# Two changes in a network of two blocks: leftover U blocks spread over the V pass, and both halves of the feed-forward activations side by side in one matmul

## The chip, the cores and the metric

The kernel runs on one core of a Trainium2 chip. The metric is the time of one execution on the device in microseconds (us). The profile is one execution taken by the hardware profiler. Engines are named as in it: PE is TensorE (matmuls; PEld its weight loads), DVE is VectorE, ACT is ScalarE, POOL is GpSimd, and SP is the engine whose queue issues most DMAs.

## What is computed

Two blocks follow one another on 256 tokens of width 1024 (the first also carries 256 context tokens in its first layer). All data is fp32.

```python
# first block, per layer (2): attention / Fourier / convolution mixer, then a PEER layer
def peer_ffn(h, w_query, sub_keys, u_tab, v_tab):      # 16384 experts, 8 heads, top 16
    ...
    s_top, i_top = lax.top_k(s, PEER_TOPK)
    ...
    best, pos = lax.top_k(cand, PEER_TOPK)
    gate = jax.nn.softmax(best, axis=-1)
    u = jnp.take(u_tab, eid, axis=0)
    act = jax.nn.gelu(jnp.einsum('chkd,cd->chk', u, hc)) * gate
    v = jnp.take(v_tab, eid, axis=0)
    return jnp.einsum('chk,chkd->cd', act, v)

# second block, per layer (2): swiglu, attention mixer, swiglu, each with norms and modulation
def swiglu(h, w_gate, w_up, w_down):                   # width 2816
    return (jax.nn.silu(h @ w_gate) * (h @ w_up)) @ w_down
```

## The kernel before

**Products in three parts.** fp32 operands are split into a high half (the value as fp32r, rounded) and a low half (the remainder). `split` (L338) does it for weights: ACT copies `raw` to `wh` (L339), DVE or POOL subtracts to give `wl` (L340). `mm3` (L369) then makes three matmuls per 128 x 128 weight block: high weight with high activation (L371), high weight with low activation (L372), low weight with high activation (L373). Weights come as pieces of 8 blocks, 512 KB, loaded by `raw` (L344) on SP's queue; four raw tiles and two of each half rotate. `linear` (L375) runs such products over output blocks m, accumulates in a PSUM tile of 512 columns of which it uses the first n, and calls `evac` for each.

**The PEER layer** (`peer`, L1181) does not gather rows for all tokens: it multiplies all experts densely and masks. In layer 0 there are 512 tokens; the first 128 are done by gathered rows (`rows_up` L1151, `rows_down` L1167, on POOL's queue and DVE), the other 384 densely. A U block is 512 experts: four quarters of 8 weight blocks, 24 matmuls of 384 columns each, with a Gelu on ACT into `a4` (two buffers in pool `pp`). While the U blocks run, the top-k search `topk` (L989) for four tiles of 128 tokens is advanced by a generator. Each of its steps has a cost; for each quarter of a U block `peer` pays it `budget` units (3.1 in layer 0) and lets it run till they are spent. Its costs: 1.0, 16 x 1.1, 4.0, 8 x 0.7, 32 x 0.75 for every tile, and 2.0 and 32 x 1.7 more for a tile that is done densely (one-hot products, tiles `oa` and `ob` on DVE, `sc` on PE, `stg` on POOL). The rows of the first tile advance by `rate["up"]` (1.22) per quarter once that tile's search is done. A block's result is written to DRAM (`ad`, ACT's queue, L1269), the gates to `gd` (L1133).

The search ends in block number nb - 1; blocks from nb on are left. The loop's own sums give 122 quarters, hence nb = 31 in layer 0.

**The V pass** follows. `prep(b)` reads the gates of block b (L1288, 768 KB in layer 0, as much as its `a`) and either reads its `a` back from DRAM (L1293, b < nb) or computes the U block there and then, multiplies, and splits the product into `w4h` and `w4l`. V blocks are then taken two at a time (`deep` = 2), eight output blocks d of 8 weight blocks (24 matmuls) each, from weights `vt`. Order of the blocks: the first one left over, then all others in their order. `prep` runs two to four blocks ahead. POOL's part of the weight splits is switched off in this pass (`self.share = 0`). `rows_down` advances by 1.15 steps for each d. The program order is only a priority: the framework's scheduler lays out each engine's order ahead of time, and each engine then runs its own list in order.

**Feed-forward** (`ffn`, L1452), four times: 44 output blocks (gate and up alternating) of 8 weight blocks, then 8 output blocks of 22. `e` takes Silu of a gate block straight from PSUM (L1463), multiplies with the up block from PSUM (L1466) and splits the product into `ah` and `al` (L1467, L1468). `out_evac` (L1394) squares and scales each output block from PSUM. In layer 0 `sums` adds modulation sums on DVE (L443), 1.4 per pair of blocks.

Of the kernel before, what the change touches and what calls it, by code (L numbers as in the profile page):

```python
# [12 lines left out]
F32R = mybir.dt.float32r  # L13
U32 = mybir.dt.uint32
I32 = mybir.dt.int32
AF = mybir.ActivationFunctionType
# [217 lines left out]
class Kernel:  # L234
# [134 lines left out]
    def mm3(self, out, wh, wl, xh, xl, start, stop):  # L369
        mm = self.nc.tensor.matmul  # L370
        mm(out, wh, xh, start=start, stop=False)  # L371
        mm(out, wh, xl, start=False, stop=False)  # L372
        mm(out, wl, xh, start=False, stop=stop)  # L373

# [611 lines left out]
    rate = {("gate", 0): (10, 0, 2), ("gate", 1): (4, 0, 2), ("u", 0): 0, ("u", 1): 0, ("v", 0): 0, ("v", 1): 1.25, "mix": (5, 1.3), "up": 1.22, "down": 1.15, "ffn": 1.4, "out": 1, "att": (0.4, 0.4), "norm": ((4,4), (2,2), (4,4), (4,4))}  # L986
# [194 lines left out]
    def peer(self, l, budget):  # L1181
# [8 lines left out]
        with ExitStack() as es:  # L1190
# [90 lines left out]
            with self.pool(f"vp{l}") as vp:  # L1281
# [59 lines left out]
                if nb < 32:  # L1341
                    order = [nb] + order[:nb] + order[nb + 1 :]
# [27 lines left out]
    def hidden(self):  # L1370
        h = self.h = self.t(self.bp, [P, 2, 8, T], "h", F32R, bufs=1)
        self.rhs = (lambda k: h[:, 0, k], lambda k: h[:, 1, k])
        return h
# [78 lines left out]
    def ffn(self, l, j, nxt):  # L1452
        nc = self.nc
        with self.banks(mm=4, sc=3), self.pool(f"fp{l}{j}") as fp:
            ah = self.t(fp, [P, NF, T], "ah", F32R)
            al = self.t(fp, [P, NF, T], "al", F32R)
# [3 lines left out]
            def e(m, ps):  # L1460
                if m % 2 == 0:
                    sg["t"] = self.t(fp, [P, T], "sg", bufs=2)
                    nc.scalar.activation(sg["t"], ps, AF.Silu)  # L1463
                else:
                    t, k = sg["t"], m // 2
                    nc.vector.tensor_tensor(t, ps, t, op=OP.mult)  # L1466
                    nc.scalar.activation(ah[:, k], t, AF.Copy)  # L1467
                    last = nc.vector.tensor_sub(al[:, k], t, ah[:, k].bitcast(F32))  # L1468
                    self.sums(self.rate["ffn"], last)
                if m == 12 and l == 0 and j == 0:  # L1470
                    self.bias_read()

            self.linear(gu, 8, range(2 * NF), self.rhs, e, lead=4)
            if l == 0 and j == 1:
                self.sums_end()
            st = self.out_begin(l, 2 * j, True)
            self.linear(
                self.stream("wdn", (2 * l + j) * NF), NF, range(8), (lambda k: ah[:, k], lambda k: al[:, k]),
                lambda d, ps: self.out_evac(st, d, ps, nxt is None),
# [177 lines left out]
    def run(self):  # L1657
# [13 lines left out]
        self.peer(0, 3.1)  # L1671
# [39 lines left out]
```

## Time and profile before

| | |
|---|---|
| median of 3 runs | 4171.94 us (4168.49 to 4172.41) |
| the profiled execution | 4176.94 us, span of its instructions 4175.2 us |
| mean granted clock of TensorE | 0.945 |
| PE busy | 3820.4 us (92%) |
| DVE busy | 3235.8 us (77%) |
| ACT busy | 1794.7 us (43%) |
| POOL busy | 968.9 us (23%) |
| DMA | 944.96 MB, mean 226 GB/s |

Where stages lie, in us from the span's start: first mixer to 490, PEER layer 0 about 500 to 1937 (U blocks and search to 1330, V pass from there), second mixer to 2200, PEER layer 1 to 3050, then the second block. Busy time of PE is modelled, and matmuls overlap by their pipeline, so the distance between the starts of two matmuls is their cost, not the duration of one. A row of waits says which engine and line waited for which.

### The profile page before, as it was taken

What the parts mean: (1) busy time and instruction counts of PE and PEld (TensorE: products, weight loads), DVE (VectorE), ACT (ScalarE), POOL (GpSimd) and SP (SyncE); (2) the same over time, 40 slices, a digit from 0 to 9 for tenths busy, and PEclk for the clock granted to TensorE, in tenths of its full rate; (3) what the DMA queues carried; (4) which work ended last, traced back from release to release, by engine and by line L of the source; (5) the groups of instructions that cost most, each with busy time, mean ns of one, the idle gap of its engine ahead of it and who ended that gap; (6) DMA issues with size and microseconds to landing.
All of it is one profiled execution on the core that took longest, in us unless ns stands there. A gap on an engine that the chain in (4) does not pass through costs nothing.

```text
span 4175.2 us, 69284 instructions
## 1 busy us (share of the span) xinstructions
PE 3820.4 (92%) x25443; PEld 3562.4 (85%) x25443; DVE 3235.8 (77%) x7950; ACT 1794.7 (43%) x2986; POOL 968.9 (23%) x803
## 2 busy tenths in 40 slices
PE   7889898978897699999899999999989989999898
PEld 5568798978786599998689999999989879998798
DVE  4768778988987699996768997898868778656664
ACT  3342333433444233333344656444444554444543
POOL 0100014654634233440302848000000010100100
PEclk9999999999896799999899999999999989999899
DMA  5436548888756999984235767999869439554244
GB/s 181 157 103 216 184 156 292 290 287 279 251 191 176 254 348 345 340 324 140 98 117 186 251 234 254 378 363 341 310 232 315 155 104 320 159 184 146 95 162 142
DMA packets 331123, 944.96 MB, mean 226 GB/s; under 512 B 30832, under 2 KB 118512, under 8 KB 330784
## 3 DMA queue, kind: packets, MB, share of 16 engines
q1 hardware_dynamic: 201776, 722.15, 49.8%
q0 software_dynamic: 38272, 137.38, 10.3%
q10 hardware_dynamic: 90736, 81.01, 5.9%
q8 instruction: 201, 3.29, 0.3%
q14 instruction: 138, 1.13, 0.1%
HBM read 855.23 MB, written 85.19 MB: 225 GB/s over the span
## 4 chain that ended last, share of the span: by engine, by line
PE 46%; DVE 8%; issue 7%; DMA 3%; ACT 1%; POOL 1%; another core or an unknown queue 1%; ACTq 0%; SPq 0%; DVEq 0%; POOLq 0%
PE mm L373 14%; PE mm L371 14%; PE mm L372 14%; DVE wl L340 2%; DMA raw<-in_vt 2%; DVE cj L1061 1%; ACT wh L339 1%; PE sc L1122 1%; DMA arow<-in_adat 1%; DMA gd<-stg 1%; DVE cacc L770 1%; DVE w4l L340 0%; DVE nu L535 0%; PE sc L510 0%
## 5 line engine op out<-in xcount | busy, mean ns | idle before, releaser
L339 ACT ACTIVATE wh<-raw 128x1024 fp32r<-128x1024 f32 x946 | 997.0, 1057 | 1535.0 <-PE mm L372 1173.3
L340 DVE TENSOR_TENSOR wl<-raw,wh 128x1024 fp32r<-128x1024 f32 x840 | 1054.6, 1259 | 446.4 <-ACT wh L339 439.2
L373 PE MATMUL mm<-h2h,wl 128*128 128x256 f32 (+2 forms) x2176 | 694.5, 320 | 61.6 <-DVE wl L340 57.2
L371 PE MATMUL mm<-h2h,wh 128*128 128x256 f32 (+2 forms) x2176 | 692.7, 320 | 20.7 <-ACT a L1238 13.8
L372 PE MATMUL mm<-h2l,wh 128*128 128x256 f32 (+2 forms) x2176 | 692.2, 318 | 0.0
L371 PE MATMUL mm<-w4h,wh 128*128 128x384 f32 (+1 forms) x2048 | 631.8, 312 | 26.0 <-ACT wh L339 25.8
L373 PE MATMUL mm<-w4h,wl 128*128 128x384 f32 (+1 forms) x2048 | 601.2, 312 | 35.2 <-DVE wl L340 35.1
L372 PE MATMUL mm<-w4l,wh 128*128 128x384 f32 (+1 forms) x2048 | 630.3, 311 | 2.3 <-DVE w4l L340 2.3
L371 PE MATMUL mm<-h,wh 128*128 128x256 f32 x1712 | 498.4, 291 | 16.5 <-ACT h L540 6.7
L372 PE MATMUL mm<-h,wh 128*128 128x256 f32 x1712 | 494.4, 289 | 2.4 <-DVE h L541 1.8
L373 PE MATMUL mm<-h,wl 128*128 128x256 f32 x1712 | 490.7, 287 | 0.5 <-DVE wl L340 0.5
L373 PEld LDWEIGHTS mm<-h2h,wl 128*128 128x128 f32 x2176 | 425.4, 196 | 74.1 <-DVE wl L340 65.3
L371 PEld LDWEIGHTS mm<-h2h,wh 128*128 128x128 f32 x2176 | 425.4, 196 | 27.8 <-ACT a L1238 16.6
L372 PEld LDWEIGHTS mm<-h2l,wh 128*128 128x128 f32 x2176 | 425.4, 196 | 2.7
L373 PEld LDWEIGHTS mm<-w4h,wl 128*128 128x128 f32 x2048 | 383.3, 191 | 42.1 <-DVE wl L340 41.8
L371 PEld LDWEIGHTS mm<-w4h,wh 128*128 128x128 f32 x2048 | 391.3, 192 | 31.2 <-ACT wh L339 30.2
L372 PEld LDWEIGHTS mm<-w4l,wh 128*128 128x128 f32 x2048 | 391.5, 191 | 2.8 <-DVE w4l L340 2.8
L371 PEld LDWEIGHTS mm<-h,wh 128*128 128x128 f32 x1712 | 335.5, 196 | 24.2 <-ACT h L540 10.4
L372 PEld LDWEIGHTS mm<-h,wh 128*128 128x128 f32 x1712 | 335.2, 196 | 9.7 <-DVE h L541 7.1
L340 POOL TENSOR_TENSOR wl<-raw,wh 128x1024 fp32r<-128x1024 f32 x106 | 260.2, 2455 | 345.2 <-ACT wh L339 332.1
L373 PEld LDWEIGHTS mm<-h,wl 128*128 128x128 f32 x1712 | 334.9, 196 | 0.7 <-DVE wl L340 0.7
L1146 POOL DMA_INDIRECT vr<-in_vg,rowid x128 | 196.0, 1531 | 375.3 <-DVE racc L1178 350.6
(356 smaller groups left out, 7413.0 us busy)
## 6 DMA issues: line engine op xcount, KB each, us to landing
raw<-in_ut SPq DMA_DIRECT2D x256, 512.0 KB
raw<-in_vt SPq DMA_DIRECT2D x256, 512.0 KB
raw<-in_wgu SPq DMA_DIRECT2D x176, 512.0 KB
arow<-in_adat SPq DMA_DIRECT2D x144, 512.0 KB
raw<-in_wdn SPq DMA_DIRECT2D x88, 512.0 KB
gd<-stg ACTq DMA_DIRECT2D x20, 2048.0 KB
raw<-in_win SPq DMA_DIRECT2D x66, 512.0 KB
raw<-in_wmod SPq DMA_DIRECT2D x48, 512.0 KB
```

The lines of the kernel that those rows point to most:

```text
L339: self.nc.scalar.activation(h, src, AF.Copy)
L340: (eng or self.nc.vector).tensor_sub(l, src, h.bitcast(F32))
L371: mm(out, wh, xh, start=start, stop=False)
L372: mm(out, wh, xl, start=False, stop=False)
L373: mm(out, wl, xh, start=False, stop=stop)
L770: nc.vector.scalar_tensor_tensor(av[:, cc], u[:, cc, :, k : k + T], w[:, cc * 31 + k : cc * 31 + k + 1], av[:, cc], op0=OP.mult, op1=OP.add,)
L1061: nc.vector.scalar_tensor_tensor(junk, self.iota[:, :NCAND], pf[:, h, k : k + 1], eid[:, h, :], op0=OP.is_equal, op1=OP.mult, accum_out=se ...
L1122: nc.tensor.matmul(pg[:, j * 256 : (j + 1) * 256], oa[:, 2 * h + j], obs[h][:, j].rearrange("p a b -> p (a b)"), start=True, stop=True,)
L1146: self.nc.gpsimd.indirect_dma_start(out=r, out_offset=None, in_=self.A[table], in_offset=bass.IndirectOffsetOnAxis(ap=ids[:, i : i + 1], a ...
```

## The change

It has two parts, and three numbers go with them.

In the PEER layer with gathered rows (layer 0) the budget per quarter goes from 3.1 to 3.9 and the rows' rate from 1.22 to 1.65. The blocks that are left when the search ends are no longer taken as "the first of them, then all in order", but sorted by their share of progress, so that they lie evenly among the others: with nb = 25 the order is 25, 0, 1, 2, 3, 26, 4, 5, 6, 7, 27, 8 and so on. Layer 1 keeps its order and its budget.

In the feed-forward networks the high and the low half of an activation block lie beside each other, [k, 2, T]. One matmul of 512 columns multiplies the high weight with both, another of 256 columns adds the low weight's product to the first half. Two halves of the PSUM tile result, and `halves` adds them: a copy of the second on ACT, an addition on DVE. Silu, the multiplication and `out_evac` then read this sum from SBUF.

```diff
+    def linear2(self, get, nk, ms, rhs, evac, lead=1):
+
+        ms = list(ms)
+        mm = self.nc.tensor.matmul
+        for grp in [ms[:lead]] + [[m] for m in ms[lead:]]:
+            pss = [self.ps("mm") for _ in grp]
+            for k in range(nk):
+                both = rhs[:, k].rearrange("p a b -> p (a b)")
+                for m, ps in zip(grp, pss):
+                    wh, wl = get(m * nk + k)
+                    mm(ps, wh, both, start=k == 0, stop=False)
+                    mm(ps[:, 0:T], wl, rhs[:, k, 0], start=False, stop=k == nk - 1)
+            for m, ps in zip(grp, pss):
+                evac(m, ps)
+
+    def halves(self, out, ps):
+        self.nc.scalar.activation(out, ps[:, T : 2 * T], AF.Copy)
+        self.nc.vector.tensor_tensor(out, ps[:, 0:T], out, op=OP.add)
+        return out
...
-    rate = {("gate", 0): (10, 0, 2), ("gate", 1): (4, 0, 2), ("u", 0): 0, ("u", 1): 0, ("v", 0): 0, ("v", 1): 1.25, "mix": (5, 1.3), "up": 1.22, "down": 1.15, "ffn": 1.4, "out": 1, "att": (0.4, 0.4), "norm": ((4,4), (2,2), (4,4), (4,4))}
+    rate = {("gate", 0): (10, 0, 2), ("gate", 1): (4, 0, 2), ("u", 0): 0, ("u", 1): 0, ("v", 0): 0, ("v", 1): 1.25, "mix": (5, 1.3), "up": 1.65, "down": 1.15, "ffn": 1.4, "out": 1, "att": (0.4, 0.4), "norm": ((4,4), (2,2), (4,4), (4,4))}
...
                 order = list(range(32))
-                if nb < 32:
+                if g0:
+                    order.sort(key=lambda b: ((b - nb) / (32 - nb), 0) if b >= nb else (b / nb, 1))
+                elif nb < 32:
                     order = [nb] + order[:nb] + order[nb + 1 :]
...
     def hidden(self):
-        h = self.h = self.t(self.bp, [P, 2, 8, T], "h", F32R, bufs=1)
-        self.rhs = (lambda k: h[:, 0, k], lambda k: h[:, 1, k])
+        t = self.hh = self.t(self.bp, [P, 8, 2, T], "h", F32R, bufs=1)
+        h = self.h = t.rearrange("p k a b -> p a k b")
+        self.rhs = (lambda k: t[:, k, 0], lambda k: t[:, k, 1])
         return h
...
-            ah = self.t(fp, [P, NF, T], "ah", F32R)
-            al = self.t(fp, [P, NF, T], "al", F32R)
+            a2 = self.t(fp, [P, NF, 2, T], "a2", F32R)
+            ah, al = a2[:, :, 0], a2[:, :, 1]
...
                 if m % 2 == 0:
-                    sg["t"] = self.t(fp, [P, T], "sg", bufs=2)
-                    nc.scalar.activation(sg["t"], ps, AF.Silu)
+                    t = sg["t"] = self.halves(self.t(fp, [P, T], "sg", bufs=2), ps)
+                    nc.scalar.activation(t, t, AF.Silu)
                 else:
                     t, k = sg["t"], m // 2
-                    nc.vector.tensor_tensor(t, ps, t, op=OP.mult)
+                    u = self.halves(self.t(fp, [P, T], "su", bufs=1), ps)
+                    nc.vector.tensor_tensor(t, u, t, op=OP.mult)
...
-            self.linear(gu, 8, range(2 * NF), self.rhs, e, lead=4)
+            self.linear2(gu, 8, range(2 * NF), self.hh, e, lead=4)
...
-            self.linear(
-                self.stream("wdn", (2 * l + j) * NF), NF, range(8), (lambda k: ah[:, k], lambda k: al[:, k]),
-                lambda d, ps: self.out_evac(st, d, ps, nxt is None),
+            self.linear2(
+                self.stream("wdn", (2 * l + j) * NF), NF, range(8), a2,
+                lambda d, ps: self.out_evac(st, d, self.halves(self.t(fp, [P, T], "su", bufs=1), ps), nxt is None),
             )
...
-        self.peer(0, 3.1)
+        self.peer(0, 3.9)
```

## Rows read from the trace of the kernel before

**Rows 1.** The page's slices: busy tenths of two engines in 40 equal slices.
```profile
PE   7889898978897699999899999999989989999898
DVE  4768778988987699996768997898868778656664
```

**Rows 2.** Busy by stretch: length, PE, PEld, DVE, ACT, POOL, PEclk, DMA, GB/s.
```profile
500.00:545.00 45.00, 43.80 (x200) 36.06 (x201) 23.34 (x70) 17.00 (x29) 0.00 (x0) 0.97 0.22 71
...
690.00:765.00 75.00, 69.79 (x382) 68.75 (x383) 63.32 (x295) 22.70 (x34) 33.09 (x26) 0.95 0.87 306
765.00:880.00 115.00, 102.88 (x592) 98.52 (x591) 114.29 (x220) 59.95 (x101) 89.69 (x94) 0.97 0.89 302
880.00:1030.00 150.00, 119.63 (x626) 116.06 (x625) 120.70 (x563) 42.45 (x61) 62.79 (x49) 0.87 0.76 263
1030.00:1150.00 120.00, 102.73 (x536) 96.01 (x535) 116.07 (x207) 52.90 (x92) 78.52 (x81) 0.90 0.79 260
...
1243.00:1312.00 69.00, 51.36 (x126) 35.42 (x127) 68.14 (x155) 38.15 (x66) 46.43 (x63) 0.53 0.41 126
...
1330.00:1440.00 110.00, 61.73 (x292) 57.58 (x291) 55.18 (x90) 22.91 (x36) 21.31 (x13) 0.77 0.97 236
1440.00:1880.00 440.00, 432.68 (x2465) 426.21 (x2464) 413.69 (x624) 152.53 (x207) 166.79 (x110) 1.00 0.93 340
...
500.00:1312.00 812.00, 708.99 (x3655) 663.75 (x3656) 713.85 (x2755) 324.27 (x510) 380.62 (x360) 0.90 0.69 233
```

**Rows 3.** Groups by line, DVE's and POOL's weight splits in 500:1312.
```profile
L340 DVE TENSOR_TENSOR wl<-raw,wh 128x1024 fp32r<-128x1024 f32 x91 | 131.0, 1440 | 38.3 <-ACT wh L339 34.2 <-PE sc L1122 3.7
...
L340 POOL TENSOR_TENSOR wl<-raw,wh 128x1024 fp32r<-128x1024 f32 x41 | 98.5, 2402 | 171.1 <-ACT wh L339 160.3 <-PE sc L1122 6.5 <-PE mm L373 3.9
```

**Rows 4.** DVE's waits in 545:1312: who for whom, total us, times, longest.
```profile
DVE ur L1159 <- DMA ur<-in_ug,rowid: 30.3, 15, 6.4
DVE top L1006 <- ACT s L1001: 16.9, 3, 10.5
DVE wl L340 <- ACT wh L339: 15.8, 15, 2.9
```

**Rows 5.** Order of time, PE, middle of the V pass: start, duration, engine, line.
```profile
1601.05 0.33 PE L373 MATMUL mm<-w4h,wl 128*128 128x384 f32 x1
...
1602.09 0.33 PE L373 MATMUL mm<-w4h,wl 128*128 128x384 f32 x1
```

**Rows 6.** DMA queues and issues in 1320:1420 (packets, MB, share), and a chain step.
```profile
q0 software_dynamic: 2728, 7.96, 60.5%
...
a<-ad SPq DMA_DIRECT2D x4, 768.0 KB
...
1335.11 38.05 DMA raw<-in_vt
```

**Rows 7.** Order of time, PE: 256 columns in feed-forward, 512 in the first mixer.
```profile
4140.08 0.28 PE L371 MATMUL mm<-ah,wh 128*128 128x256 f32 x1
...
4141.49 0.28 PE L371 MATMUL mm<-ah,wh 128*128 128x256 f32 x1
...
69.65 0.39 PE L371 MATMUL mm<-hs,wh 128*128 128x512 f32 x1
...
72.37 0.39 PE L371 MATMUL mm<-hs,wh 128*128 128x512 f32 x1
```

**Rows 8.** Groups by line over the span: Silu from PSUM, product from PSUM.
```profile
L1463 ACT ACTIVATE sg<-mm 128x256 f32<-128x256 f32 x88 | 32.3, 367 | 1.7 <-DVE al L1468 1.7
L1466 DVE TENSOR_TENSOR sg<-mm,sg 128x256 f32<-128x256 f32 x88 | 37.2, 423 | 37.5 <-PE mm L373 35.8 <-ACT sg L1463 1.4
```

**Rows 9.** Busy by stretch, gate and up blocks of the first feed-forward network.
```profile
3070.00:3196.00 126.00, 124.30 (x1026) 124.10 (x1025) 97.59 (x145) 59.36 (x87) 0.00 (x0) 0.99 0.82 283
```

**Rows 10.** Order of time: the end of the last network.
```profile
4162.22 0.28 PE L373 MATMUL mm<-ah,wl 128*128 128x256 f32 x1
4162.54 0.38 ACT L482 ACTIVATE sq<-mm 128x256 f32<-128x256 f32 x1 [7.02 <-PE mm L373]
```

## Prediction, made before the changed kernel ran

> **What bounds the kernel now.** I read the page's slices first [rows 1]: TensorE (PE) is nearly full everywhere except in the stretch that holds the first PEER layer, and there VectorE (DVE) is full instead. So the second view is the table by stretches over that layer [rows 2]. Up to 1312 us the U blocks (PE) run beside the top-k search and the one-hot products (DVE). In 500:1312 DVE is busy for 713.85 of 812 us; where one-hots are built (765:880, 1030:1150, 1243:1312) it has nothing left, and PE pauses. The reader should see 1243:1312 above all: no U block is left, PE does 126 small matmuls at a granted clock of 0.53, DVE 68.14 of 69 us. This stage is DVE's. In the V pass it is the other way round: 1440:1880 holds 2465 matmuls, which at 0.1733 us each (seven starts from 1601.05 to 1602.09 of [rows 5]: 1.04 / 6) are 427 of 440 us. The V pass belongs to PE, although DVE (413.69 us) and the DMA engines (0.93) are near their ends too. Only its first 110 us, 1330:1440, are loose: 292 matmuls, some 51 us of work. There the queue of software descriptors holds 60.5% of the DMA engines and a load of V weights takes 38.05 us [rows 6]. In the feed-forward stages PE runs without a gap, a 256-column matmul every 0.1175 us [rows 7].
>
> **The change part by part: U blocks.** The loop over U blocks pays 3.1 units of top-k cost per quarter block. The costs in the code sum to 378 (52.2 for the first token tile, 3 x 108.6 for the others), so 122 quarters, 31 whole blocks, are run before the search ends, and one is left. At 3.9 it is 97 quarters, 25 blocks: seven are left, six more than before, and in layer 0 alone (the other layer keeps its budget).
>
> V pass. Six blocks x 4 pieces x 24 matmuls of 384 columns x 0.1733 us = **+99.8 us** of PE, in a stage where PE is the bound. What of it could vanish: the 13 us that PE is short in 1440:1880, and some of the 59 us in 1330:1440, since a U block asks for 2 MB of weights alone per 16.6 us of PE, a V block for 2 MB and twice 768 KB. But all new blocks but the first stand behind V work in program order, and that work itself waits for V weights; so I take 10 us back, and 40 as the end of the range. A moved block's instructions: its four loads go into SP's queue between V's loads; its write-out on ACT's queue and its read-back on SP's fall away (12 transfers of 768 KB in all); four copies and four Gelus join ACT, which is a third busy here (152.53 of 440 us), so they are covered; the four subtractions all go to DVE, since POOL's share is off in this pass: 4 x 1.2 = 5 us beside 16.6 us of PE, which loosens DVE (94% now) rather than loads it. It also adds a wait: a U block holds one of two a4 buffers while it is computed, and the read-back of a later block, with V's loads behind it on SP, waits for that. Two buffers and two blocks of lead make me take 0; the upper end is one piece of PE, 4.2 us, for each of six blocks, 25 us. Sum: **+90, between +60 and +125**.
>
> U stage. What DVE loses is its part of 24 subtractions: it does 91 of 132 for 131.0 us [rows 3], so 24 x 0.69 x 1.44 = 24 us, and 690 us stay. How much of its idle 98 us goes is the question that decides the sign. Some 22 us lie in 500:545, where the query projection keeps PE full and no search can start; 16.9 are the first step of a search waiting for its scores, which recurs per tile [rows 4]. These stay. Of 30.3 us that wait for gathered rows a third should go, as fewer U weights share the DMA engines; the 15.8 behind ACT's copies, which wait for PE to free weights, should mostly go, and about half of the remainder. I take 69 us of idle, a stage of 759: **-53**. The ends: idle stays as it is, -24; only the 39 fixed microseconds stay, 690 + 39 = 729, -83. The faster pace of row products (1.65 per quarter) moves the same 128 products into fewer quarters and costs nothing, because DVE has to do them in this stage in any case: by the loop's sums they end in quarter 91 of 100; were they late, they would drain before V, at 1.3 us each.
>
> Layer 0 together: +90 - 53 = **+37 us, from -23 to +101**.
>
> **Feed-forward.** The products of the high weights with both halves of the activations become one 512-column matmul; a third weight load of each triple goes, but loads are hidden behind matmuls already. PE gains only what an issue costs beside its columns: 2 x 0.1175 against one of 512 columns, 2.72 us for twelve starts from 69.65 to 72.37 [rows 7], 0.2267: 8.3 ns. There are 2112 such triples (four networks x (44 x 8 + 8 x 22)), so **-17.5 us**. The Trainium skill, TensorE: Matmul & The Clock Gate, section Back-to-back issue gap, gives N / 2.4 + 2.5 ns for a matmul of N columns at full clock. By that a triple would gain 2.5 ns, and all of them 5 us; this trace's matmuls show a larger fixed part, and the trace decides.
>
> Each output block now needs a copy on ACT and an addition on DVE, at most 0.37 and 0.42 us by their neighbours [rows 8], 52 per network. On ACT (59 of 126 us busy in the first network [rows 9]) they are covered. On DVE they are in layer 1; in the two networks of layer 0, where the modulation sums run too, DVE goes from 97.59 to about 115 of some 123 us. That is still under PE, but DVE keeps to its order and weight halves will come late now and then: 3 us, from 0 to 12 (both networks). At the end of each network nothing covers the pair: after the last matmul the square starts at once [rows 10], and copy, addition and two hand-overs come before it, about 0.95 us x 4 = +4. Feed-forward: **-10.5, from -18 to +6**.
>
> Sum: +37 - 10 = **+27 us**. The profiled execution took 4176.94 us around a span of 4175.2, 5 us above the median of 4171.94; the difference is laid on the median: **4199 us**.
>
> **The rivals.** First, faster: the U stage closes nearly all of DVE's idle time (-83) and the start of the V pass takes in a good part of the new blocks (+60), with feed-forward at -11: -34, 4138 us. For it: outside the one-hot stretches DVE stands at 80 to 85% (690:765, 880:1030) because PE holds it up there, and a larger share of search per block is what would fill that. Against it: it needs both ends at once; it decides from 80 us recovered in U and V together. Second, an even trade: the U stage gives 75, V costs 85: +10 - 11, about 4171 us. Third, much slower: U blocks already run ahead of the search, so that 69 us of one-hots stand alone at the end; with a quarter fewer blocks they end sooner, the lone tail grows, PE's clock falls there as it does in 1243:1312, and the stage gives DVE's 24 us alone: +90 - 24 - 6 = +60, and with late read-backs +85, 4232 to 4257 us. For it: DVE's total is fixed and its waits for gathered rows and first scores have nothing to do with PE. Fourth, layer 0 as forecast but no more than 5 us from the merged matmul, because a 512-column issue between shorter ones may not keep the spacing that it has among its like: +37 - 5 + 7 = +39, 4211 us; the skill's rule above would have it so, the rows don't.
>
> **How the numbers follow.** Forecast 0.42, first rival 0.28, second 0.12, third 0.13, fourth 0.05. Faster by over 0.2% (8 us, about what can be told apart here) is the first rival: 0.28; within, the second: 0.12; slower, the others: 0.60. Cases of both signs hold weight, so the forecast's own range stands apart: 4182 to 4222. The 8-in-10 range cuts a tenth on either side: it runs from the first rival's 4138 to the middle of the third, 4246.
>
> **What would show it.** In the changed profile: 25 write-outs of a in layer 0 instead of 31, the U stage (first query matmul to last one-hot) at 760 us rather than 812, V's matmuls from first to last at about 700 rather than 607 us. The prediction is wrong if the U stage falls to 730 or below, if V grows by less than 70, or if the feed-forward stages of layer 0 lengthen. A 512-column matmul followed by one of 256 should take 0.344 us a pair.

## The result, and the profile after

| | before | after |
|---|---|---|
| median of 3 runs | 4171.94 us (4168.49 to 4172.41) | 4205.03 us (4197.96 to 4210.09) |
| the profiled execution | 4176.94 us, span 4175.2 us | 4197.96 us, span 4196.2 us |
| mean granted clock of TensorE | 0.945 | 0.947 |

The ratio is 1.0080, with a 95% interval from 1.0055 to 1.0105: the changed kernel is 33 us slower by the medians, 21 us by the two profiled spans (that of after is the shortest of its three runs). In the rest of the text the stages of layer 0 are cut like this: the U stage runs from the first matmul of the query projection to the last one-hot matmul, the V pass from the first matmul with V weights to the token sum that closes the layer. The table is made from the starts of these matmuls in the two traces.

| stage (us) | before | after | difference |
|---|---|---|---|
| up to the first query matmul | 500.2 | 503.9 | +3.7 |
| U stage | 811.0 | 752.6 | -58.4 |
| between U stage and V pass | 18.5 | 18.0 | -0.5 |
| V pass | 610.0 | 703.0 | +93.0 |
| second mixer and PEER layer 1 | 1113.7 | 1111.4 | -2.3 |
| second block | 1121.7 | 1107.3 | -14.4 |

So layer 0 became 34.1 us longer and the second block 14.4 us shorter. The first view to read is the table by stretches of after (length, PE, PEld, DVE, ACT, POOL, PEclk, DMA, GB/s; busy us and instructions):

```profile
503.90:1257.00 753.10, 606.70 (x3078) 558.48 (x3079) 687.11 (x2738) 288.58 (x459) 366.96 (x351) 0.88 0.68 229
1128.00:1257.00 129.00, 57.99 (x148) 39.87 (x147) 124.12 (x636) 43.87 (x76) 47.24 (x64) 0.53 0.30 90
1274.50:1360.00 85.50, 38.88 (x174) 34.88 (x173) 34.84 (x57) 15.04 (x25) 12.07 (x8) 0.72 0.99 211
1360.00:1960.00 600.00, 593.36 (x3408) 589.29 (x3407) 500.79 (x733) 211.28 (x286) 171.49 (x121) 1.00 0.83 290
```

The first line answers to 500:1312 of [rows 2]: DVE does 687 us of work in 753 us, where it did 714 in 812. Its idle time fell from 98 to 66 us. The second line answers to 1243:1312 there. No U block is left from 1128 on, and the stretch without one has grown from 69 to 129 us, at a granted clock of 0.53. The last tile's one-hots take no more of it than before (68.3 us against 68.9 from first to last); what is new is that the search ahead of them stands alone as well. DVE is busy in 124 of the 129 us, so it loses little there. The third line is the head of the V pass, as empty as before (174 matmuls in 85.5 us with the DMA engines at 0.99), and in the fourth PE is full: 3408 matmuls at 0.1733 us are 591 of 600 us.

What DVE lost is seen in its groups of weight splits in 503.9:1257 (they answer to [rows 3]), and what it still waits for in its table of waits from 549 on ([rows 4]):

```profile
L340 DVE TENSOR_TENSOR wl<-raw,wh 128x1024 fp32r<-128x1024 f32 x75 | 107.0, 1426 | 26.9 <-ACT wh L339 26.8
L340 POOL TENSOR_TENSOR wl<-raw,wh 128x1024 fp32r<-128x1024 f32 x33 | 79.1, 2398 | 112.1 <-ACT wh L339 110.8 <-PE sc L1142 0.8
```
```profile
DVE ur L1179 <- DMA ur<-in_ug,rowid: 24.5, 23, 2.7
DVE wl L340 <- ACT wh L339: 7.5, 4, 3.5
DVE top L1026 <- ACT s L1021: 6.4, 2, 4.0
```

75 splits in place of 91 take 107.0 in place of 131.0 us: the 24 us of the prediction. The V pass shows the moved blocks as matmuls from `h2h` among those from `w4h` (groups by line in 1274.5:1977.5):

```profile
L371 PE MATMUL mm<-w4h,wh 128*128 128x384 f32 x1024 | 345.5, 338 | 22.6 <-ACT wh L339 22.6
...
L373 PE MATMUL mm<-w4h,wl 128*128 128x384 f32 x1024 | 324.4, 338 | 26.9 <-DVE wl L340 26.9
...
L371 PE MATMUL mm<-h2h,wh 128*128 128x384 f32 x192 | 64.2, 334 | 0.0
```

192 is six blocks of 32 high-weight products; the seventh block that is left over runs before the first V matmul, in the 18 us between the stages. PE's idle time before V's own products (22.6 and 26.9 us, split weights that came late) lies almost all in the head. The DMA queues and issues in 1270:1370, the stretch that answers to [rows 6], say why:

```profile
q0 software_dynamic: 2895, 8.58, 61.2%
...
a<-ad SPq DMA_DIRECT2D x4, 768.0 KB, 30.9
dd<-bv POOLq DMA_DIRECT2D x2, 1532.0 KB, 64.4
```

The software queue carries two writes `dd<-bv` that take 64 us to land, beside gathered rows. By bytes the writes are 3.1 of its 8.58 MB, but an experiment below shows that the hole in PE's work goes with them. They are the table of attention biases for the second block (`bias_write`, called in the V loop at i = 8, but laid at its start by the scheduler): 8 partitions hold a row each, which is written 128 times, 1532 bytes at a time. While they run a read-back of `a` takes 30.9 us, and the head of the pass moves 211 GB/s (third line of the first fence), where the pass moves 290 later on.

In the feed-forward networks the order of time on PE shows pairs in place of triples (after, the last network: first its gate and up blocks, then its down blocks):

```profile
4029.12 0.39 PE L385 MATMUL mm<-h,wh 128*128 128x512 f32 x1
4029.35 0.28 PE L386 MATMUL mm<-h,wl 128*128 128x256 f32 x1
4029.47 0.39 PE L385 MATMUL mm<-h,wh 128*128 128x512 f32 x1
...
4169.95 0.40 PE L385 MATMUL mm<-a,wh 128*128 128x512 f32 x1
4170.18 0.28 PE L386 MATMUL mm<-a,wl 128*128 128x256 f32 x1
4170.30 0.39 PE L385 MATMUL mm<-a,wh 128*128 128x512 f32 x1
```

A pair takes 0.35 us in both, where the prediction had 0.344. In the kernel before, a triple of the down blocks took 3 x 0.1175 = 0.3525 [rows 7]. One of the gate and up blocks took 0.36: between these two starts lie 17 steps, (4010.87 - 4008.83) / 17 = 0.120 each (kernel before, order of time, last network):

```profile
4008.83 0.28 PE L372 MATMUL mm<-h,wh 128*128 128x256 f32 x1
...
4010.87 0.28 PE L371 MATMUL mm<-h,wh 128*128 128x256 f32 x1
```

Whole runs are surer than single starts; these are the last network's, from the operation views of the two kernels (count, least/median/longest ns, first and last start), before and then after:

```profile
L371 PE MATMUL mm<-h,wh x352: 278/283/582, 3969.1 to 4099.8; 128*128 128x256 f32 x176
L373 PE MATMUL mm<-h,wl x352: 278/283/415, 3970.2 to 4100.0; 128*128 128x256 f32 x176
L371 PE MATMUL mm<-ah,wh x176: 280/280/282, 4100.1 to 4162.0; 128*128 128x256 f32 x176
L373 PE MATMUL mm<-ah,wl x176: 279/279/279, 4100.4 to 4162.2; 128*128 128x256 f32 x176
```
```profile
L385 PE MATMUL mm<-h,wh x352: 390/391/792, 3994.3 to 4120.6; 128*128 128x512 f32 x176
L386 PE MATMUL mm<-h,wl x352: 277/280/415, 3994.9 to 4120.9; 128*128 128x256 f32 x176
L385 PE MATMUL mm<-a,wh x176: 391/392/399, 4121.0 to 4182.2; 128*128 128x512 f32 x176
L386 PE MATMUL mm<-a,wl x176: 278/280/286, 4121.2 to 4182.4; 128*128 128x256 f32 x176
```

From first to last start the gate and up blocks went from 130.9 to 126.6 us, the down blocks from 62.1 to 61.4. Over the four networks the first kind gained 3.9, 2.9, 3.2 and 4.3 us, the second 0.0, 0.0, 0.7 and 0.7: 14.3 and 1.4. At the end of each network the added copy and addition stand in the open (after, order of time, the last network; before: [rows 10]):

```profile
4182.39 0.28 PE L386 MATMUL mm<-a,wl 128*128 128x256 f32 x1
4183.05 0.38 ACT L391 ACTIVATE su<-mm 128x256 f32<-128x256 f32 x1 [6.26 <-PE mm L386]
4183.47 0.42 DVE L392 TENSOR_TENSOR su<-mm,su 128x256 f32<-128x256 f32 x1 [6.62 <-ACT su L391]
4183.92 0.42 ACT L502 ACTIVATE sq<-su 128x256 f32<-128x256 f32 x1 [0.49 <-DVE su L392]
```

The square starts 1.53 us behind the last matmul's start, where it started 0.32 us behind it.

### The profile page after: what moved, and what is told of

The parts are those of the page before. It is cut to its first block, busy times and chain, and to the rows that moved or that the text cites. A ratio compares the mean times of both kernels' runs of the same rounds, so it can differ in the third digit from the quotient of the medians.

```text
span 4196.2 us, 65291 instructions
## 1 busy us (share of the span) xinstructions
PE 3784.3 (90%) x23331; PEld 3429.4 (82%) x23331; DVE 3307.7 (79%) x8166; ACT 1861.1 (44%) x3194; POOL 946.4 (23%) x795
## 3 DMA queue, kind: packets, MB, share of 16 engines
q0 software_dynamic: 38272, 137.38, 10.2%
## 5 line engine op out<-in xcount | busy, mean ns | idle before, releaser
L340 DVE TENSOR_TENSOR wl<-raw,wh 128x1024 fp32r<-128x1024 f32 (+1 forms) x848 | 1057.6, 1249 | 436.4 <-ACT wh L339 434.2
L385 PE MATMUL mm<-h,wh 128*128 128x512 f32 x1408 | 504.7, 403 | 15.1 <-DVE h L561 7.1
L386 PE MATMUL mm<-h,wl 128*128 128x256 f32 x1408 | 398.7, 283 | 0.0
L385 PEld LDWEIGHTS mm<-h,wh 128*128 128x128 f32 x1408 | 268.5, 191 | 83.2 <-DVE sg L392 7.6
L340 POOL TENSOR_TENSOR wl<-raw,wh 128x1024 fp32r<-128x1024 f32 x98 | 240.8, 2457 | 285.3 <-ACT wh L339 281.9
L1149 POOL TENSOR_TENSOR stg<-s 128x256 f32<-128x256 f32 x320 | 267.3, 859 | 146.5 <-ACT s L1147 85.3
L1166 POOL DMA_INDIRECT vr<-in_vg,rowid x128 | 185.8, 1452 | 446.4 <-DVE racc L1198 424.7
L1131 DVE SCALAR_TENSOR_TENSOR ob<-io,top,ix 128x256 fp32r<-128x256 f32 x640 | 267.1, 472 | 12.9 <-PE sc L1142 11.9
L386 PEld LDWEIGHTS mm<-h,wl 128*128 128x128 f32 x1408 | 270.4, 192 | 0.0
## 6 DMA issues: line engine op xcount, KB each, us to landing
gd<-stg ACTq DMA_DIRECT2D x20, 2048.0 KB, 13.1
```

Source lines behind the costliest of these rows:

```text
L340: (eng or self.nc.vector).tensor_sub(l, src, h.bitcast(F32))
L385: mm(ps, wh, both, start=k == 0, stop=False)
L386: mm(ps[:, 0:T], wl, rhs[:, k, 0], start=False, stop=k == nk - 1)
L1131: nc.vector.scalar_tensor_tensor(ob[:, j], iota.unsqueeze(1).to_broadcast([P, 2, P]), ij[:, 1, t : t + 1], ghl[:, t].unsqueeze(2).to_broad ...
L1149: nc.gpsimd.tensor_tensor(stg[:, :, c : c + 2].rearrange("p b t -> p t b"), both[:, :, 0], both[:, :, 1], op=OP.add)
L1166: self.nc.gpsimd.indirect_dma_start(out=r, out_offset=None, in_=self.A[table], in_offset=bass.IndirectOffsetOnAxis(ap=ids[:, i : i + 1], a ...
```

## The experiments

A time here is a median; a ratio is that to the kernel before as it ran beside the experiment, with its 95% interval, and stages are read from one profiled execution each. The theory was the prediction's own: the V pass belongs to PE and pays 16.6 us for a moved block, the U stage belongs to DVE and gives back DVE's splits and some of its idle time, and the feed-forward gain is PE's alone. The rivals: the moved blocks cost more than their matmuls (their place in the order, a wait of their own, loads), and the head of the V pass is what decides.

**The two parts alone.** First the U part without the feed-forward part (e1: the edits to `rate["up"]`, the order and the budget), then the feed-forward part without the U part (e2).

> Only the U-block part of the change (budget 3.9, rows' rate 1.65, the leftover blocks sorted among the others); the feed-forward networks stay as before. Theory (V pass owned by PE, U stage by DVE): the changed kernel's layer-0 PEER layer took 34.1 us longer from its first query matmul to its last token sum (1473.6 against 1439.5 us), so this alone should be +30 to +40 us over before, 4202 to 4212 us, with the first V matmul about 55 us earlier and the V pass about 90 us longer than before. Rival (layer 0 is about even and the rest of the program pays): within 10 us of before.

> Only the feed-forward part (one 512-column matmul for both halves, the sum of two PSUM halves); budget, rate and order as before. Theory (a triple of matmuls gains 8.3 ns, the ends lose about 0.95 us each, DVE in the layer with modulation sums takes a little back): -8 to -14 us, each network of layer 1 shorter by 3 to 4.5 us, each of layer 0 by 1 to 3.5 us. Rival (an issue costs 2.5 ns, so that a triple gains 2.5 ns and the ends eat it): 0 to +5 us, no network shorter by more than 1 us.

Measured: 4221.07 us (4216.65 to 4225.17), ratio 1.0117 [1.0093, 1.0140], for the U part; 4152.69 us (4147.95 to 4156.93), ratio 0.9958 [0.9939, 0.9976], for the feed-forward part. The product of the two, 1.0075, is the ratio of the whole change (1.0080) within its interval: no sign that the parts touch each other. By the profile of the first the U stage is 751.3 and the V pass 712.7 us, by that of the second the second block is 1110.8 us (1121.7 before). The loss is the U part's. It is larger than expected, 49 us by the ratio where 30 to 40 were named; and the feed-forward part gains 17.5 us by its ratio (10 to 25 by the interval), where 8 to 14 were named. Only 7.9 us of that lie in the four networks of its profile; its U stage, which the part doesn't touch, is 14.8 us shorter than in the kernel before, and that is the spread of this stage (see below).

**How many blocks.** The U part alone with other budgets, which leave four and eleven blocks to the V pass (e3: 3.5 with a rows' rate of 1.45; e4: 4.7 with 2.0):

```diff
-        self.peer(0, 3.9)
+        self.peer(0, 3.5)
```

> The U-block part at half the dose: budget 3.5 and rows' rate 1.45, so that 28 blocks are run beside the search and four are left, three more than before. Theory: V gains 3 x 15 = 45 us; the U stage gives back DVE's 12 us and the easily freed part of its idle time, 20 to 30 us together: +10 to +22 us. Rival (a threshold: up to some number, moved blocks fill holes for nothing, and only the last of them cost): 0 or faster, down to -20 us.

> The U-block part at a higher dose: budget 4.7 and rows' rate 2.0, so that 21 blocks are run beside the search and eleven are left, ten more than before. Theory: V gains 10 x 15 = 150 us; the U stage gives 53 us as at six blocks and then little more than DVE's 4 us per block, 70 us in all: +80 us (65 to 95). Rival (the U stage shrinks with its blocks, 9 us for each): 150 - 90 = +60 us or less. Second rival (V does not lengthen by PE's full work, since DVE and DMA were its real bound): below +45 us.

Measured: 4175.68 us (4162.06 to 4182.77), ratio 1.0011 [0.9995, 1.0027], and 4260.10 us (4252.86 to 4265.09), ratio 1.0212 [1.0187, 1.0237]. The table by stretches of each, the U stage alone:

```profile
503.50:1268.00 764.50, 660.58 (x3365) 611.71 (x3366) 699.26 (x2746) 307.13 (x484) 373.99 (x355) 0.90 0.70 237
```
```profile
503.60:1243.00 739.40, 559.16 (x2693) 505.11 (x2694) 667.80 (x2727) 268.64 (x427) 344.12 (x346) 0.83 0.65 217
```

With the first line of after this makes a series. DVE works 714, 699, 687 and 668 us with one, four, seven and eleven blocks left; it idles 98, 65, 66 and 72 us. The first three moved blocks take away all the idle time that goes at all; every block after them gives DVE's splits, 4 us a block, or less (the stage shrinks by 11.8 us for the next three and 13.4 for the next four, DVE's work by 12.2 and 19.3). The V pass grows by 53.1, 93.0 (102.7 in the U part alone) and 123.2 us for three, six and nine blocks in it, 14 to 18 us a block, about the 16.6 us of their matmuls; with eleven left a second block lies ahead of the pass, and the time between the stages is 49.4 us rather than 18. Hence the first three come out about even and all others lose. The expectation for four left (+10 to +22) lies above the measured +5 us (-2 to +11 by the interval), since it had 20 to 30 us from the U stage and the profile has 47; its rival foresaw the even result, but not the reason, for the V pass took the blocks in at their full price. The expectation for eleven (+65 to +95) held: +88 by the ratio.

How sure the idle time is can be read from the other kernels on this page. With one block left and the same settings the U stage took 811.0, 796.2, 809.1, 802.8 and 807.0 us and DVE idled 85 to 97 us; with seven left it took 751 to 755 us in five profiles and DVE idled 65 to 67 us. So the floor is firm, and the first three blocks took 20 to 32 us of idle time, by which profile they are compared with.

**The order.** The U part (e5) with the old order of blocks, the first one left over and then all in their order, so that six U blocks come one after another at the end of the V pass:

```diff
-                if g0:
-                    order.sort(key=lambda b: ((b - nb) / (32 - nb), 0) if b >= nb else (b / nb, 1))
-                elif nb < 32:
+                if nb < 32:
                     order = [nb] + order[:nb] + order[nb + 1 :]
```

> Budget 3.9 and rows' rate 1.65 as in the run with the U-block part alone (4221 us, +52 over before), but the old order of blocks: 25, then 0 to 24, then 26 to 31 at the end of the V pass. Theory (V is owned by PE, so a moved block costs its matmuls wherever it stands): within 12 us of that run, +40 to +64 over before. Rival (the cost comes from breaking V's streams, so that sorted blocks cost more than a closed run at the end): faster than that run by 20 us or more. Rival (the spread is what keeps the cost down, since DVE and DMA get relief all along): slower than it by 15 us or more, as the end would be U blocks alone and the stretch before as tight as it was.

Measured: 4209.07 us (4207.19 to 4218.63), ratio 1.0097 [1.0076, 1.0118], against 1.0117 for the spread order; the V pass is 705.3 us, against 712.7. Where the blocks lie makes no difference that can be told apart: the V pass of one and the same spread order is 703.0 in the whole change and 712.7 in the U part alone. Spreading the blocks neither hides their matmuls nor costs anything that shows.

**PE or not.** The U part (e6), with the third product of each left-over U block left out; `self.two` is set while such a block is computed:

```diff
         mm(out, wh, xh, start=start, stop=False)
-        mm(out, wh, xl, start=False, stop=False)
-        mm(out, wl, xh, start=False, stop=stop)
+        mm(out, wh, xl, start=False, stop=stop and self.two)
+        if not self.two:
+            mm(out, wl, xh, start=False, stop=stop)
...
+                    self.two = b >= nb and g0 > 0
                     src = None if b < nb else list(ublock(4 * b))
+                    self.two = False
```

> The U-block part alone, but each leftover U block leaves out its third product (low weight with high activation) in all layers' dense PEER code where a block is computed inside V of layer 0: 7 x 32 matmuls of 384 columns, 38.8 us of PE at 0.1733 us; loads, splits and everything else stay. Theory (V pass owned by PE): 30 to 39 us faster than the run with the U-block part alone, the V pass shorter by that. Rival (V bound by DVE's or the DMA engines' work, the U blocks' matmuls fit in between): less than 10 us faster.

Measured: 4191.61 us (4185.37 to 4193.61), ratio 1.0058 [1.0037, 1.0079], 25 us less than the U part by the ratios (1.0117 - 1.0058, of 4167). The V pass is 686.8 us, 25.9 less, for 192 matmuls less, 33.3 us. Loads, copies and splits are as many as before: three quarters of what was taken from PE came off the pass (half, if it is held against the 703.0 of the whole change). That is less than the 30 to 39 us expected and more than the rival's 10, so it is PE that pays for the larger part. The rest came back as waits. PE's idle time in the V pass is 58.6 us in the U part and 66.6 us here, and the largest row of it is V's own third product, waiting for split weights (groups by line in the V pass, U part alone, then this run):

```profile
L373 PE MATMUL mm<-w4h,wl 128*128 128x384 f32 x1024 | 325.6, 339 | 32.2 <-DVE wl L340 32.2
```
```profile
L374 PE MATMUL mm<-w4h,wl 128*128 128x384 f32 x1024 | 328.1, 340 | 44.2 <-DVE wl L340 44.1
```

The U blocks' own third product waited 3.2 us for its weights in the U part alone, so what leaving it out saved beside matmuls is small.

**The head of the V pass.** The feed-forward part (e7), then the whole change (e8), with the table write of the bias, its small loads and two small matmuls taken out of the V pass and put at the start of the second mixer:

```diff
+                if l == 1:
+                    self.bias_write(mp, *self.bias_load(mp))
...
-                bias = self.bias_load(vp) if l == 0 else None
...
-                    if l == 0 and i == 8:
-                        self.bias_write(vp, *bias)
```

> Only the feed-forward part, and the relative-position table's write to DRAM (two DMAs of 1532 KB on POOL's queue that landed after 64 us at the head of the V pass and held 60% of the DMA engines) moved to the second mixer, with its three loads and two small matmuls. Theory (V's head stands still for that write): the head of V, where PE has some 50 us of work in 110, closes by 35 to 50 us; the second mixer, whose DMA engines are a third busy, pays 0 to 10: 4105 to 4125 us. Rival (the head waits for the gathered rows and for the gates' read-back in any case): 4145 to 4155 us, as with the feed-forward part alone.

> The whole change, and the table's write moved to the second mixer as in the run beside it. Theory: the same 35 to 50 us as there, 4150 to 4170 us, so that the change stays dearer by about 45 us than the feed-forward part alone under the same move. Rival (leftover blocks cost as much as they do because one of them falls into the write at V's head): the gap between the two closes to 25 us or less.

Measured: 4130.87 us (4123.24 to 4139.39), ratio 0.9905 [0.9878, 0.9932], and 4197.30 us (4187.19 to 4208.41), ratio 1.0077 [1.0052, 1.0102]. The next lines are the head of the V pass in the first and the head of its second mixer (table by stretches), the software queue in that second stretch (DMA queues), and the head of the second mixer in the kernel before:

```profile
1331.80:1440.00 108.20, 102.28 (x578) 99.60 (x577) 103.28 (x164) 40.12 (x59) 40.16 (x23) 1.00 0.99 380
...
1880.00:1960.00 80.00, 43.93 (x216) 33.44 (x216) 21.01 (x47) 17.34 (x33) 3.67 (x4) 0.70 0.77 73
```
```profile
q0 software_dynamic: 1184, 3.14, 68.0%
```
```profile
1940.00:2020.00 80.00, 73.19 (x442) 60.10 (x442) 58.16 (x126) 34.75 (x65) 18.24 (x10) 0.88 0.33 106
```

In the first kernel the V pass starts at full pace and is 545.9 us long, 64 less than in the feed-forward part alone. The hole goes with the write: the second mixer is 312.5 us (269.5 there), where 0 to 10 us more were expected, so of the 64 us some 21 are left. With the write gone from V, six blocks cost it 658.6 - 545.9 = 112.7 us, and the U stage gives 57.6: hardly another loss than before, so the head stall was no reason for it. In layer 0 the change costs 54 us without the stall (1428.1 - 1373.7) and 49 with it (1473.6 against 1424.7 of the feed-forward part alone).

The second kernel missed its expectation (4150 to 4170 us): 1.0077 is the ratio of the whole change as it was. The V pass is 44.4 us shorter, and the second mixer and PEER layer 1 together are 45 us longer. By the ratios the two kernels of this experiment lie 72 us apart, where 45 were expected; the rival's 25 us or less are further off.

A table over the V passes (matmuls of U and V weights counted in the traces, PE's part at 0.1733 us each):

| kernel | blocks computed in V | matmuls | PE's part | V pass | remainder |
|---|---|---|---|---|---|
| before | 0 | 3072 | 532 | 610.0 | 78 |
| four left | 3 | 3360 | 582 | 663.1 | 81 |
| after | 6 | 3648 | 632 | 703.0 | 71 |
| U part alone | 6 | 3648 | 632 | 712.7 | 81 |
| U part, old order | 6 | 3648 | 632 | 705.3 | 73 |
| eleven left | 9 | 3936 | 682 | 733.3 | 51 |
| feed-forward part, write moved | 0 | 3072 | 532 | 545.9 | 13 |
| whole change, write moved | 6 | 3648 | 632 | 658.6 | 26 |

The remainder hangs on where the write is, and little on the number of blocks up to six. With eleven left it is smaller, but there the write is issued at 1265.7, 27 us before the pass starts, so that part of it falls between the stages, beside the second block that lies there. With the write moved, six blocks add 13 us to the remainder; 8 of them are waits of PE, mainly for split weights (17.8 us of idle time against 9.7).

**No block left over.** The first kernel with the write moved, and a budget of 3.0 (e9), with which the search ends in the last U block:

> The feed-forward part and the moved table write, as in e7, with a budget of 3.0 for a quarter of a U block: the search then ends in the last of the 32 blocks and none is left for the V pass (e7 leaves one). If a left-over block costs V what the runs so far showed (112.7 us for six between e7 and e8, 18.8 each) and saves the U stage 57.6 / 6 = 9.6, the pass back gives V -19 and U +10: about -9 us against e7, 4122 us. Rival: with only one block left, the block lies first in V, where the first V weights are still on their way, and costs nothing there; then only the U stage grows and the time is 4141 us.

Measured: 4149.81 us (4136.56 to 4162.56), ratio 0.9961 [0.9942, 0.9979]. The V pass is 546.0 us, as with one block (545.9): that block is free, as the rival has it, because it runs in the gap in which the last gates are written and read back (18.7 us with it, 21.6 without). The U stage, which both expected 10 us longer, is 799.6 in the profile, 9 us shorter, while the ratio is 0.0056 above that of the kernel with one block, 23 us, and the time is above both expectations. The two profiles can't show where those went, because they are only 3.5 us apart (4142.90 and 4139.39 us, the longest of the four runs of the kernel with one block); this stays open.

**Less DVE work in the U stage.** The feed-forward part with the write moved, but every second weight split on POOL in place of every third (e10):

```diff
-    shares = (3, 2)
+    shares = (2, 2)
```

> e7 with every second weight split of layer 0's U stage on POOL instead of every third. DVE loses some 24 of its 91 splits at 1.44 us, 35 us; POOL gains 24 at 2.4 us, 58 us on 381 of 812. If DVE bounds the U stage, as the prediction has it, the stage becomes 20 to 35 us shorter than the 808 us of e7, with as many U blocks as there: about 4105 us. If a moved split only puts its time on POOL, whose splits are 1.0 us slower and lie in the same chain from the load to the matmul, the stage stays within 10 us of 808 or lengthens: 4130 us or more.

Measured: 4135.29 us (4122.56 to 4142.81), ratio 0.9929 [0.9907, 0.9952]. In the profile DVE does 70 splits and POOL 62 (91 and 41), DVE's work falls by 21.8 us, and the U stage by 17, from 809.1 to 791.7; the time, taken over all runs, is no better than 0.9905 [0.9878, 0.9932]. The table of waits shows a part of what was given back:

```profile
DVE ob L1133 <- PE sc L1144: 16.8, 11, 5.7
```

The wait of the one-hots for PE was 4.8 us. A gain of 17 us in one profile is about what the U stage varies by itself: 796 to 811 us in the five profiles with the same settings. So this experiment settles nothing; whether DVE's work alone sets the length of the U stage is not shown by it.

**A better place for the write.** With the feed-forward part, the write at the start of layer 1's U stage (e11); and, in its old place, on ACT's queue of hardware descriptors in place of POOL's (e12, the edit below):

```diff
-            nc.gpsimd.dma_start(
+            nc.scalar.dma_start(
```

> e7 with the table write not in the second mixer but at the start of layer 1's U stage, behind its query projection. The write keeps the DMA engines for some 64 us wherever it stands; the question is whether a stage has loads that can wait so long. In V of layer 0 it cost 64 us (e2 against e7), in the second mixer 43. If layer 1's U stage, where DVE has a search of its own to run and PE need not have its weights at once, covers it: V 546 us as in e7, mixer 266 us as in e2, PEER layer 1 within 10 us of 845, total 4090 us. Rival: U weights come at half pace there too, PE falls behind and nothing fills it up again: PEER layer 1 is 30 to 60 us longer, 4120 to 4150 us, no better than e7.

> The feed-forward part alone, as e2, with the two table writes (1532 KB each, from 8 partitions) issued on ACT's hardware queue in place of POOL's software queue, in the same place of the code. If the stall at the head of V belongs to the software queue, the writes land in well under 64 us, or take a smaller share beside the loads, and V is up to 64 us shorter: V 546 to 580 us, 4090 to 4125 us. If it belongs to the shape of the transfer (8 partitions, 1532-byte rows), the write holds the engines as long: V 600 us or more, about 4150 us, and ACT's write-outs of a wait behind it besides.

Measured: 4140.61 us (4130.89 to 4150.62), ratio 0.9931 [0.9907, 0.9955], and 4137.96 us (4128.09 to 4152.24), ratio 0.9928 [0.9910, 0.9945]. In the first, V is 547.1 us, the second mixer 269.6, and PEER layer 1 888.2, 47 us longer than in the feed-forward part alone (841.4): the rival. In the second, V is 587.0 us, 23 less than with the software queue and between the two expectations. So the queue has a part. What the other 41 us over 545.9 belong to isn't shown: the shape of the transfer is one candidate, and ACT is another, since one of the two issues stood for 14.5 us on its queue, and PE waited once 13.1 us for a copy of ACT's. All three ways come to nearly the same time, 0.7 to 1% under the kernel before. The write in the second mixer has the lowest ratio (0.9905) and lies clear of the feed-forward part alone (0.9958); its interval overlaps those of the other two, so that it is the best of the three isn't shown.

## Why the prediction was right, step by step

**What bounds the stages.** DVE the U stage, PE the V pass. The third product's removal shows the second for the moved blocks: half to three quarters of the matmul time that was taken away came off the pass, and the rest came back mainly as waits for split weights. The first is argued and not shown. For it speak DVE's 124 of 129 us in the stretch without U blocks, and the series of budgets, in which the stage shrinks beyond three moved blocks by no more than DVE's splits. The one experiment that took work from DVE alone stayed within the spread of the stage.

**V pass, +90 (60 to 125).** Measured +93.0, and +102.7 with the U part alone. The 99.8 us of PE are there (576 more matmuls). The 10 us that the start of the pass should give back came as 7 in the one and not at all in the other, within the 10 us by which the pass varies. The reason given (all new blocks but the first stand behind V work that waits for weights) fits the head of after, which is as empty as before. The wait for an `a4` buffer, taken at 0, doesn't show while the write lies in the pass: the remainder is no longer with six blocks than with none. With the write moved it is 13 us longer, 8 of them waits of PE, mainly for split weights, a term that the sum didn't have.

**U stage, -53 (-24 to -83).** Measured -58.4; DVE's work 687 us (690 foretold), its idle time 66 (69), the stage 753 us from the first query matmul (759 of 812 from 500 on). Over the profiles with one block left (805 us in the mean of five) and with seven (753), it is -52.5. The sum was right, its parts less so: waits for gathered rows fell from 30.3 to 24.5 us, not by a third; those behind ACT's copies halved, from 15.8 to 7.5; those for a search's scores, which were to stay, fell from 16.9 to 6.4. The last two are no clean effect of the change: with one block left, the feed-forward part alone has 6.0 and 6.4 us for them too. Which waits fill the idle time differs from run to run; its sum is the steadier figure.

**Layer 0, +37.** Measured +34.1; +42.9 in the profile of the U part alone. Of the signs that were named, the 25 write-outs of `a`, the U stage near 760 and the V pass near 700 are there; the pair of matmuls takes 0.35 us in place of 0.344.

**Feed-forward, -10.5 (-18 to +6).** Measured -14.4 for the second block, -11.8 for the four networks from their first matmul to their token sum. Over all profiles on this page, eight with the merged matmuls and six without, the networks are shorter by 10.2 us in the mean. The stated range isn't the sum of its terms: -17.5 with 0 to 12 on DVE and +4 at the ends gives -13.5 to -1.5. PE gained 14.3 + 1.4 = 15.7 us, 17.5 foretold, but not as foretold: 10.1 ns for each of the 1408 triples of gate and up blocks, 2.0 ns for each of the 704 of the down blocks, where the sum had 8.3 for all. The step took a row of down blocks (0.1175) and one of the first mixer (0.2267) for all of them. In the kernel before the gate and up matmuls started every 0.120 us, which those rows don't show; and a 512-column matmul followed by one of 256 takes 0.230 us. That the total came out near is luck: one kind gained more than the sum had, the other less. For the down blocks the fourth rival was right. The 2.5 ns a triple that the prediction took from the Trainium skill, TensorE: Matmul & The Clock Gate, section Back-to-back issue gap, are near the 2.0 measured there; but the Trainium skill gives that formula for an isolated matmul, and an estimate by it is 0.109 us for 256 columns, where the trace has 0.1175. So the nearness bears out no rule for these streams. For the gate and up blocks, with 10.1 ns, the trace disagrees with the rival and with the formula. What made them slower before wasn't tried. DVE's 3 us don't show (the first network, where DVE is fullest, gained 3.9 us on its gate and up blocks, as much as the others); the ends cost 1.2 us in the last network, from the last matmul to the token sum (1.21 before, 2.45 after), and 0.8 to 0.9 us in the other three, 3.9 in all, for 4 foretold.

**Sum, +27.** Measured +21.0 between the profiled spans, +33.1 between the medians. The stages that the change doesn't touch moved by +3.7, -0.5 and -2.3 us, which is the noise of such a comparison. By the ratios of the two parts alone the U part costs more than its +37 (49 us) and the feed-forward part gives more than its -10.5 (17.5 us); that the sum came out nearer than its terms is in part luck.

**The rivals.** The first needed 80 us from U and V together; it got 58 + 7 = 65. The second wanted 75 from U: the idle time has a floor of some 65 us, which no budget tried went under. The third saw rightly that the lone tail would grow (69 to 129 us) and the granted clock fall there (0.53), and was wrong that this is a loss: DVE is busy in 124 of the 129 us, and its one-hot operation `ob` takes 0.47 us there as it does beside a U block. What counts there is DVE's idle time in the whole stage, and it fell.

**What was seen and not followed up.** The prediction's own rows held another stall as long as a stage's gain: the software queue's 60.5% in the head of the V pass [rows 6]. It took them as given. Behind them stands one table write, which costs the pass 64 us; moving it to the second mixer, on top of the feed-forward part, took the ratio from 0.9958 to 0.9905. On top of the whole change it brought nothing that shows (1.0080 and 1.0077).

## What to carry to other kernels

In this kernel, work moved from a stage that one engine fills to a stage that another fills was paid nearly in full where it arrived, and returned only what it took of the first stage's fullest engine, plus idle time down to a floor; so price both ends by their bounding engine, and stop at the block where the floor is reached. A stall with full DMA engines and little data moved asks for the name of the transfer that fills them: read the issues of that stretch, with their time to landing, before costing anything that is to be hidden there. And take the spacing of matmuls from the very line that is to be changed, since two lines of one shape may differ.

## What the runs showed of the hardware

Two writes of 1532 KB each, from 8 partitions in rows of 1532 bytes, took 64 to 68 us to land on the software queue and cost the stage where they fell 64 us (V pass), 43 us (second mixer) or 47 us (PEER layer 1). In the second mixer's head that queue carried nothing else (3.14 MB) and held 68% of the DMA engines, which moved 73 GB/s, against 380 GB/s in the V pass with its ordinary loads of 512 KB. On ACT's hardware queue the V pass lost 23 us less. And matmuls of one shape, 128 x 256, started every 0.1175 us in one stage and every 0.120 in another, both with PE full; no run shows the cause.
